# Splitting the first load of a transfer-bound attention-score kernel, and fixed buffers in place of a rotating pool

## The chip, the cores and the metric

The kernel runs on one core of one Trainium2 chip. The metric is the device time of one execution in microseconds; a profile gives, besides, the span from the first to the last instruction, which is about 1.8 us shorter than that time.

## The reference

```python
batch, heads, seq, dim = 8, 8, 512, 64
q, k = float32 [8, 8, 512, 64]
scores = np.einsum('bhqd,bhkd->bhqk', q, k) * (1 / sqrt(64))     # float32 [8, 8, 512, 512]
```

8.4 MB of q and 8.4 MB of k are read, and 67.1 MB of scores are written.

## The kernel before

Four pairs of batches are loaded at the start, k then q, each as one transfer of 128 partitions with 16 KB each (a packet, in what follows, is one such contiguous run). GpSimd casts them to bfloat16 in two halves, TensorE transposes them, and for each pair four output tiles of 4 MB are made by matmuls, evacuated from PSUM (copied out of the buffer into which the matmuls write) by ScalarE and VectorE in turn, and stored. Loads and output tiles share one pool of three buffers of 32 KB a partition.

```python
    big_pool = ctx.enter_context(tc.tile_pool(name="big", bufs=3))
    ...
    def load_and_cast(v):
        xf = big_pool.tile([P, 2, 2, J * D], f32, name="big")
        for x, src in enumerate((k_r, q_r)):
            nc.sync.dma_start(out=xf[:, x], in_=src[v].rearrange("p (s c) -> p s c", s=2))
        for x in range(2):
            xb = bf_pool.tile([P, JP, 2, D, 2], bf16, name="xb")
            for s in range(2):
                pinned(nc.gpsimd.tensor_copy(out=xb[:, :, s]..., in_=xf[:, x, s]...))
    ...
    def scores(v, t):
        o = big_pool.tile([P, 2, RO, S], f32, name="big")
        ...   # 2 x 4 x 2 matmuls, each pair evacuated into o
        nc.sync.dma_start(out=out_r[v, t], in_=o.rearrange("p x i k -> p x (i k)"))
    ...
    cast = [load_and_cast(v) for v in range(UNITS)]        # UNITS = 4: all loads first
```

## Time and profile before

| | before |
|---|---|
| time, median of 6 runs | 202.47 us (202.37 to 202.51) |
| span of the profiled run | 200.7 us |
| transfers: share of the span that the queue's packets took | 98.3% |
| VectorE, TensorE, ScalarE, GpSimd busy | 53%, 52%, 42%, 20% |

Read it from the transfer row: one engine class is full and nothing else is near. The lines themselves stand in the prediction below. "The transfers" are 16 engines side by side, and a share or a GB/s in these views is their mean.

### The profile page before, as it was taken

What the parts mean: (1) busy time and instruction counts of PE and PEld (TensorE: products, weight loads), DVE (VectorE), ACT (ScalarE), POOL (GpSimd) and SP (SyncE); (2) the same over time, 40 slices, a digit from 0 to 9 for tenths busy, and PEclk for the clock granted to TensorE, in tenths of its full rate; (3) what the DMA queues carried; (4) which work ended last, traced back from release to release, by engine and by line L of the source; (5) the groups of instructions that cost most, each with busy time, mean ns of one, the idle gap of its engine ahead of it and who ended that gap; (6) DMA issues with size and microseconds to landing.
All of it is one profiled execution on the core that took longest, in us unless ns stands there. A gap on an engine that the chain in (4) does not pass through costs nothing.

```text
span 200.7 us, 1143 instructions
## 1 busy us (share of the span) xinstructions
PE 105.3 (52%) x384; PEld 45.8 (23%) x384; DVE 106.8 (53%) x98; ACT 85.0 (42%) x97; POOL 39.5 (20%) x22
## 2 busy tenths in 40 slices
PE   0035758566657465478637496748585667510000
PEld 0034535223214131224313122312121111100000
DVE  6705538486475976485749357844444444630000
ACT  2004423864755629253844384366435243620000
POOL 1299999995000000000000000000000000000000
PEclk9999576999699999957999759975858858975555
DMA  6999999999999999999999999999999999999994
GB/s 206 424 444 437 421 421 441 434 395 421 434 424 441 428 431 431 433 426 434 431 428 424 434 441 424 431 431 434 424 431 434 431 424 431 428 437 428 428 428 199
DMA packets 5509, 83.95 MB, mean 418 GB/s; under 512 B 384, under 2 KB 384, under 8 KB 384
## 3 DMA queue, kind: packets, MB, share of 16 engines
q1 hardware_dynamic: 5504, 83.89, 98.3%
q8 instruction: 3, 0.05, 0.1%
q14 instruction: 2, 0.02, 0.0%
HBM read 16.78 MB, written 67.11 MB: 418 GB/s over the span
## 4 chain that ended last, share of the span: by engine, by line
DMA 40%; DVE 10%; PE 8%; ACT 6%; issue 1%; ACTq 0%; SPq 0%; DVEq 0%
DMA out_dram<-big 40%; DVE big L68 9%; PE ps L141 8%; ACT big L66 5%; ACT qz L103 1%; DVE qz L103 1%; ACTq L66 0%; SPq L146 0%; DVEq L68 0%
## 5 line engine op out<-in xcount | busy, mean ns | idle before, releaser
L141 PE MATMUL ps<-kT,qz 128*128 128x512 bf16 x256 | 87.6, 447 | 55.5 <-ACT big L66 41.6
L68 DVE TENSOR_SCALAR big<-ps 128x1024 f32<-128x1024 f32 x64 | 78.4, 1224 | 59.8 <-PE ps L141 37.2
L66 ACT ACTIVATE big<-ps 128x1024 f32<-128x1024 f32 x64 | 65.5, 1023 | 73.0 <-PE ps L141 37.2
L141 PEld LDWEIGHTS <-qz 128*128 128x128 bf16 x256 | 27.2, 106 | 111.0 <-issue 97.5
L89 POOL CAST xb<-big 128x2048 bf16<-128x2048 f32 x16 | 38.8, 2468 | 7.9 <-DMA big<-in_k_dram 7.3
L117 PE MATMUL tp<-identity,xb 128*128 128x128 f32 x64 | 11.6, 346 | 13.4 <-POOL xb L89 13.4
L103 ACT COPY kT<-tp 64x512 f32<-64x512 f32 x16 | 9.2, 577 | 15.3 <-PE tp L117 15.1
L103 DVE COPY kT<-tp 64x512 f32<-64x512 f32 x16 | 11.0, 686 | 6.3 <-PE tp L117 6.0
L117 PEld LDWEIGHTS tp<-identity,xb 128*128 128x128 f32 x64 | 10.5, 184 | 15.2 <-POOL xb L89 13.4
L103 DVE COPY qz<-tp 64x512 f32<-64x512 f32 x16 | 11.0, 687 | 2.7 <-PE tp L125 2.5
L103 ACT COPY qz<-tp 64x512 f32<-64x512 f32 x16 | 9.6, 602 | 2.9 <-PE tp L125 2.7
L125 PE MATMUL tp<-identity,xb 128*128 128x128 f32 x64 | 9.4, 300 | 2.5 <-ACT kT L103 2.5
L125 PEld LDWEIGHTS tp<-identity,xb 128*128 128x128 f32 x64 | 8.5, 156 | 4.3 <-issue 3.3
L156 DVE MEMSET qz<- 128x4096 uint32 x2 | 6.9, 3472 | 2.5 <-PEq L184 1.7
L103 ACT ACT_TABLE_LOAD x1 | 1.3, 1283 | 0.7 <-PEq L184 0.7
masks.py:199 POOL TENSOR_SCALAR_AFFINE_SELECT identity<-identity 128x128 f32<-128x128 f32 x1 | 0.3, 292 | 0.1
masks.py:197 POOL MEMSET identity<- 128x128 f32 x1 | 0.2, 204 | 0.3 <-POOLq L184 0.3
L184 POOL MEMSET const-float32-0.0<- 128x1 f32 x1 | 0.1, 98 | 0.2 <-issue 0.2
L184 POOL MEMSET const-bfloat16-1.0<- 128x1 bf16 x1 | 0.1, 101 | 0.0
L184 POOL MEMSET const-uint8-127<- 128x1 uint8 x1 | 0.1, 101 | 0.0
L184 POOL MEMSET const-float32-1.0<- 128x1 f32 x1 | 0.1, 98 | 0.0
## 6 DMA issues: line engine op xcount, KB each, us to landing
out_dram<-big SPq DMA_DIRECT2D x16, 4096.0 KB, 20.7
big<-in_k_dram SPq DMA_DIRECT2D x4, 2048.0 KB, 18.1
big<-in_q_dram SPq DMA_DIRECT2D x4, 2048.0 KB, 22.7
```

What stands on the lines that cost most here:

```text
L66: pinned(nc.scalar.mul(out=dst, in_=src, mul=scale))
L68: pinned(nc.vector.tensor_scalar(out=dst, in0=src, scalar1=scale, scalar2=None, op0=mybir.AluOpType.mult))
L89: pinned(nc.gpsimd.tensor_copy(out=xb[:, :, s].rearrange("p (g i) d e -> p g e i d", i=wide), in_=xf[:, x, s].rearrange("p (g e i d) -> p ...
L103: pinned(copy(out=dst(s, h), in_=src[:, h]))
L117: pinned(nc.tensor.transpose(out=tp[:, j, :], identity=identity, in_=kb[:, j0 + j]))
L125: pinned(nc.tensor.transpose(out=tp[:, i, jj, :], identity=identity, in_=qb[:, RO * jj + i0 + i]))
L141: pinned(nc.tensor.matmul(out=ps[:, w, :], lhsT=qz[:, i + w, n, :], rhs=kT[:, n].rearrange("d m s j -> d (m s j)"), start=True, stop=True))
L156: nc.vector.memset(qz, 0.0)
L184: nc = _bacc.Bacc("TRN2", target_bir_lowering=False, num_devices=1)
```

## The change

The intent was to let the first cast start after half of the first k load, and to replace whole-slot release by dependences on parts of fixed buffers.

```diff
-    big_pool = ctx.enter_context(tc.tile_pool(name="big", bufs=3))
...
+    n_big = 0
+    def next_big():
+        nonlocal n_big
+        n_big += 1
+        return bigs[(n_big - 1) % 3]
...
-        xf = big_pool.tile([P, 2, 2, J * D], f32, name="big")
+        xf = next_big().rearrange("p (x s c) -> p x s c", x=2, s=2)
         for x, src in enumerate((k_r, q_r)):
-            nc.sync.dma_start(out=xf[:, x], in_=src[v].rearrange("p (s c) -> p s c", s=2))
+            halves = src[v].rearrange("p (s c) -> p s c", s=2)
+            for s in (slice(0, 1), slice(1, 2)) if v == x == 0 else (slice(0, 2),):
+                nc.sync.dma_start(out=xf[:, x, s], in_=halves[:, s])
...
-        o = big_pool.tile([P, 2, RO, S], f32, name="big")
+        o = next_big().rearrange("p (x i k) -> p x i k", x=2, i=RO)
...
+    bigs = [consts.tile([P, 2 * RO * S], f32, name=f"big{n}") for n in range(3)]
```

## The prediction

> **What bounds the kernel now.** I read the page first, its row of slices and its queue table, because a chain of waits has meaning only once one knows whether any engine is full.
>
> ```profile
> span 200.7 us, 1143 instructions
> ...
> DMA  6999999999999999999999999999999999999994
> GB/s 206 424 444 437 421 421 441 434 395 421 434 424 441 428 431 431 433 426 434 431 428 424 434 441 424 431 431 434 424 431 434 431 424 431 428 437 428 428 428 199
> ...
> q1 hardware_dynamic: 5504, 83.89, 98.3%
> ...
> HBM read 16.78 MB, written 67.11 MB: 418 GB/s over the span
> ```
>
> The transfers are full in 38 of 40 slices, and one queue fills 98.3% of the span. No compute engine is above 53%. The traffic is what the reference needs: both inputs once (16.78 MB), the output once (67.11 MB). The change alters none of it. To see what the two open slices hold, I asked for a table of stretches (length, matmul busy time, granted clock, DMA share, GB/s):
>
> ```profile
> core 0: us, PE busy (x), PEclk, DMA share, GB/s
> 0.00:10.00 10.00, 0.00 (x0) 1.00 0.81 315
> 10.00:40.00 30.00, 17.48 (x75) 0.83 1.01 432
> 40.00:50.00 10.00, 6.05 (x31) 1.00 1.01 416
> 50.00:100.00 50.00, 32.22 (x126) 0.90 1.01 430
> 100.00:150.00 50.00, 33.07 (x113) 0.80 1.01 431
> 150.00:195.00 45.00, 16.46 (x46) 0.69 1.01 430
> 195.00:200.70 5.70, 0.00 (x0) 0.50 0.53 227
> ```
>
> The rate is 430 to 432 GB/s wherever the queue is fed. The first 10 us move 3.15 MB, which at 430 is 7.3 us of work: the transfers start, in effect, at 2.7 us. The last 5.7 us move 1.29 MB, 3.0 us of work: they stop, in effect, at 198.0, and 2.7 us of completion and closing waits follow. 40 to 50 us lacks 14 GB/s for 10 us, 0.14 MB or 0.33 us, where loads give way to stores. So the span is 2.7 + 83.95/0.430 (195.2) + 2.7 = 200.6 us against 200.7 measured; the 1.7 us up to the 202.44 us of the timed runs lies outside the span. Only 2.7 us at the front, 0.3 us in the middle and 2.7 us at the end are not transfer.
>
> The chain that ended last and the queue's own waits look different, and would mislead if read alone:
>
> ```profile
> SPq L146 <- DVE big L68: 152.5, 16, 17.6
> SPq L195 <- DMA out_dram<-big: 21.2, 3, 9.6
> SPq L83 <- DMA big<-in_q_dram: 9.5, 1, 9.5
> SPq L83 <- POOL xb L89: 4.9, 1, 4.9
> ```
>
> The issuing queue waits 152.5 us for evacuations, yet each store takes 20.7 us from issue to landing (median, issue table), while its 4.19 MB need 9.75 us at 430 GB/s. About 11 us of that is queueing behind the store before it. The evacuations in turn wait for stores to free a buffer. This is a loop throttled by the transfers, not a slow producer.
>
> **What the Trainium skill says.** "DMA: Bandwidth & Descriptors", section Specifications, puts the ceiling of a core's 16 DMA engines at 435 GB/s, and "Perfetto Trace Analysis", section Roofline, says that a core running alone is bounded by those engines and not by its share of HBM. The trace agrees: 430 to 432 GB/s, with nothing to win above it. The DMA page, section Anatomy of one DMA, makes a transfer's fixed cost (about 2 us, on the GpSimd path) mainly completion latency, not setup; here transfers queued behind one another run at 432 GB/s, so it shows only at the ends. "SBUF — State Buffer", section SBUF: two separate sides, says that VectorE in a two-port mode and GpSimd lock each other out of a shared port for a whole instruction. That matters because GpSimd's casts will now start during VectorE's second memset. In the trace before, cast and memset overlap by 0.8 us (8.58 to 9.40) without either being longer (memset 3.47 us like the first; casts 2447 to 2491 ns), so I expect no lockout.
>
> **The change, part by part.** The opening, from the timeline:
>
> ```profile
> 0.74 0.39 SPq L83 DMA_DIRECT2D big<-in_k_dram  x1
> 1.18 0.42 SPq L83 DMA_DIRECT2D big<-in_q_dram  x1
> ...
> 8.58 34.34 POOL L89 CAST xb<-big 128x2048 bf16<-128x2048 f32 x14 [7.28 <-DMA big<-in_k_dram]
> 13.44 3.28 PEld L117 LDWEIGHTS tp<-identity,xb 128*128 128x128 f32 x16 [13.44 <-POOL xb L89]
> ```
>
> *Split load.* One more issue on the queue, 0.44 us, at 1.2 us, while 1.05 MB (2.44 us) is already queued: hidden. 128 packets of 16 KB become 256 of 8 KB, plus 16 completion packets: 144 more. I estimate 0.1 us from the footnote on the DMA page (Bandwidth section: about 10.5 ns a packet at the floor): 144 x 10.5 ns = 1.5 us, over 16 engines 0.09 us. The first cast moves from 8.58 to about 8.58 - 2.44 = 6.1 us, the second to 8.6 and its end to 11.1 (13.4 before). The q tile, however, lands at 13.4 us before (the queue's 9.5 us wait that follows its issues, which end at 3.9) and still does. GpSimd, which ran without a pause from 8.58 to 42.9, will stop from 11.1 to 13.4, and all its later casts stay put. The k transposes start 2.3 us earlier. The q transposes, which began at 19.61 after the k copies, can begin when q is cast, near 18.4: the first score product comes about 1.2 us earlier, not 2.4. None of it is on the transfer path.
>
> *Persistent buffers.* Three rotating 32 KB buffers before, the same three in the same rotation after, so the capacity in flight is unchanged. What changes is the grain of the dependences: a pool slot is released as a whole, a fixed tile by the part accessed. The built program shows it. The first evacuation into the second buffer waited for all four casts of batch pair 1 (28.13 us in the trace); now it waits for its two k casts, which end near 23.2. The fourth k load waits for the k casts alone, so it can issue near 11 to 13 us instead of 18.33; but six loads of 2.1 MB keep the queue full until 2.7 + 12.6/0.430 = 32 us, so either time is early enough. The first store should leave near 33 instead of 36.81, the second near 43 instead of 47.49, the third near 53 instead of 56.55. The loads end at 2.7 + 16.78/0.430 = 41.7, so even before the first store was 4.9 us early, and the second, needed by 41.7 + 9.75 = 51.5, 4.0 us early. More slack, zero time. After that each store waits for a buffer that the transfers free every 9.75 us, as before. Most evacuations now carry one more wait, on something long past: some tens of ns against 9.75 us per output tile, of which evacuation needs about 8 to 9 (four of 1.02 us on ScalarE beside four of 1.22 us on VectorE, with products between), and 11 us of queue lie in front of it.
>
> Sum: +0.1 for packets, 0 for the split's lead, -0.05 at the turn from loads to stores if it is touched at all, 0 for steady state: 202.44 + 0.05, which I round to 202.4.
>
> **Rivals.** (1) *The head start reaches the end*: 2.4 us of earlier work ends the program 1.2 to 2.4 us sooner, 200.0 to 201.2. For it: the first cast does start with a 7.28 us wait on that load. Against it: the queue is full from 2.7 to 198.0 us; earlier stores only queue longer. (2) *The dip at 40 to 50 us is a late store*, and earlier stores close it: -0.33 us, 202.1. Against: both stores were issued 4 us ahead, so I read the dip as the turn from reads to writes. (3) *Small packets hurt where the queue is empty*: the first packets start with no queue behind them, and the split may lose up to 0.5 us there: 202.9. (4) *The extra waits slow the refill* until a store comes late: it would take over 10 us per tile; at 1 us per tile still nothing. A full loss of 0.3 us on each of 16 stores would be 207, but nothing in the profile speaks for it.
>
> **Range and chances.** The known terms are tenths of a microsecond, the three runs before spread over 0.10 us, and 2% is 4.05 us, more than the front and the middle gap hold together (3.0 us). Rivals 2 and 3 set the range: 201.9 to 202.9. Faster by 2%: 0.01; slower: 0.01; within: 0.98.
>
> **What would show it.** Right: queue share about 98%, 430 GB/s between 50 and 195 us, first cast near 6.1, a GpSimd pause until about 13.4, first store 3 to 5 us earlier, its time to landing longer by as much, last store issued within 0.5 us of 178.1. Wrong: a stretch under 425 GB/s after 50 us (a starved queue), a first packet stretch of clearly under 315 GB/s, or an end of transfers before 197 us, which would mean that the transfer path itself got shorter.

## The result, and the profile after

The changed kernel took 203.31 us (median of 6 runs, 202.74 to 203.79) against 202.47 us (6 runs, 202.37 to 202.51): ratio 1.0043, with a 95% interval of 1.0024 to 1.0061. A ratio here is the mean time of one kernel's fast runs over that of the other's fast runs in the same rounds, so it isn't quite the ratio of the medians. The change is within 2%, as forecast, but it is slower by more than the noise, and outside the stated range of 201.9 to 202.9. Not only the median moved: the six runs spread over 1.05 us, against 0.14 us before.

The profiled run happened to be the fastest of the six (202.74 us, span 200.9). Its page, the rows of slices, packets and queue:

```profile
DMA  6999999999999999999999999999999999999994
GB/s 205 447 427 434 427 434 424 431 372 440 424 431 427 442 424 432 424 437 431 424 431 434 431 434 434 427 427 431 437 431 431 424 434 427 434 421 434 434 431 192
DMA packets 5653, 83.95 MB, mean 418 GB/s; under 512 B 400, under 2 KB 400, under 8 KB 400
...
q1 hardware_dynamic: 5648, 83.89, 98.3%
```

The queue is as full as before. The 5648 packets are 144 more than 5504: 128 for the split and 16 completion records. The ninth slice (40 to 45 us) reads 372 GB/s, where it read 395. The table of stretches, with the same columns as before, says the same:

```profile
0.00:10.00 10.00, 0.00 (x0) 1.00 0.84 324
10.00:40.00 30.00, 18.02 (x86) 0.94 1.01 430
40.00:50.00 10.00, 6.36 (x28) 1.00 0.98 403
50.00:100.00 50.00, 30.35 (x113) 0.86 1.01 431
...
195.00:200.90 5.90, 0.00 (x0) 0.50 0.54 230
```

The front is better than before (324 against 315 GB/s: 0.09 MB, or 0.2 us at 430). The stretch from 40 to 50 us is worse (403 against 416 GB/s: 0.13 MB, or 0.3 us). From 50 to 195 us the rates agree within 1 GB/s. The timeline of the start (start, duration, engine, operation, and the wait in brackets):

```profile
6.10 4.92 POOL L98 CAST xb<-big 128x2048 bf16<-128x2048 f32 x2 [4.80 <-DMA big<-in_k_dram]
...
11.04 0.33 SPq L92 DMA_DIRECT2D big<-in_k_dram  x1
...
13.45 29.46 POOL L98 CAST xb<-big 128x2048 bf16<-128x2048 f32 x12 [2.44 <-DMA big<-in_q_dram]
...
18.34 3.45 PE L134 MATMUL tp<-identity,xb 128*128 128x128 f32 x16 [3.60 <-POOL xb L98]
...
23.20 0.61 PE L150 MATMUL ps<-kT,qz 128*128 128x512 bf16 x2 [1.41 <-DVE qz L112]
...
33.72 17.43 SPq L155 DMA_DIRECT2D out_dram<-big  x3
```

The compute engines did get their head start: first cast at 6.10 us in place of 8.58, a pause of 2.44 us until q lands, first store at 33.72 in place of 36.81. None of it shortened the transfers. And the queue's waits look like before, which again tells nothing:

```profile
SPq L155 <- DVE big L66: 154.4, 16, 15.0
```

So the trace of the fast run explains 0.1 to 0.2 us, and shows a place to look: the turn from loads to stores near 41 us. What the slow runs add had to come from further traces.

**Two measures.** The Trainium skill ("DMA: Bandwidth & Descriptors", section "Why a DMA increments its semaphore by 16 and not by 1") states that a transfer's engines finish independently, and that its semaphore counts them. The page of the profile agrees: 384 packets under 512 bytes before are 24 transfers times 16. These records carry times, so from the packet records of each trace one can read when each of the 16 engines finished each transfer (a record doesn't name its engine). I use two numbers from them:

- *Loss at the last load*: the mean of the 16 finish times of the last load, less that of the load before it, less 4.87 us, which is the spacing of the early loads. Before: 42.24 - 36.98 - 4.87 = 0.39, or 0.40 us with more digits.
- *Lag*: the finish of the slowest engine in the last store, less the mean of the 16. Before: 199.48 - 198.33 = 1.15 us.

The execution ends with the slowest engine: time less its finish is 2.9 to 3.3 us in every trace.

### The profile page after: what moved, and what is told of

Read it like the earlier page. It is cut to its first block, busy times and chain, and to the rows that moved or that the text cites. A ratio compares the mean times of both kernels' runs of the same rounds, so it can differ in the third digit from the quotient of the medians.

```text
span 200.9 us, 1212 instructions
## 1 busy us (share of the span) xinstructions
PE 103.3 (51%) x384; PEld 44.7 (22%) x384; DVE 106.8 (53%) x98; ACT 85.1 (42%) x97; POOL 39.6 (20%) x22
## 3 DMA queue, kind: packets, MB, share of 16 engines
q1 hardware_dynamic: 5648, 83.89, 98.3%
## 4 chain that ended last, share of the span: by engine, by line
DMA 52%; PE 8%; DVE 8%; ACT 6%; issue 1%; ACTq 0%; SPq 0%; DVEq 0%
DMA out_dram<-big 52%; PE ps L150 8%; DVE big L66 7%; ACT big L64 6%; DVE qz L112 1%; DVE kT L112 1%; ACTq L64 0%; SPq L155 0%; DVEq L66 0%
## 5 line engine op out<-in xcount | busy, mean ns | idle before, releaser
L150 PE MATMUL ps<-kT,qz 128*128 128x512 bf16 x256 | 86.6, 440 | 60.6 <-ACT big L64 47.1
L98 POOL CAST xb<-big 128x2048 bf16<-128x2048 f32 x16 | 38.9, 2469 | 8.1 <-DMA big<-in_k_dram 4.8
L126 PE MATMUL tp<-identity,xb 128*128 128x128 f32 x64 | 10.3, 319 | 11.1 <-POOL xb L98 11.1
L126 PEld LDWEIGHTS tp<-identity,xb 128*128 128x128 f32 x64 | 9.4, 169 | 12.5 <-POOL xb L98 11.1
L134 PE MATMUL tp<-identity,xb 128*128 128x128 f32 x64 | 9.7, 306 | 3.6 <-POOL xb L98 3.6
L134 PEld LDWEIGHTS tp<-identity,xb 128*128 128x128 f32 x64 | 8.8, 161 | 5.2 <-POOL xb L98 4.0
L165 DVE MEMSET qz<- 128x4096 uint32 x2 | 6.9, 3472 | 2.5 <-PEq L194 1.7
```

The lines of the kernel that those rows point to most:

```text
L98: pinned(nc.gpsimd.tensor_copy(out=xb[:, :, s].rearrange("p (g i) d e -> p g e i d", i=wide), in_=xf[:, x, s].rearrange("p (g e i d) -> p ...
L126: pinned(nc.tensor.transpose(out=tp[:, j, :], identity=identity, in_=kb[:, j0 + j]))
L134: pinned(nc.tensor.transpose(out=tp[:, i, jj, :], identity=identity, in_=qb[:, RO * jj + i0 + i]))
L150: pinned(nc.tensor.matmul(out=ps[:, w, :], lhsT=qz[:, i + w, n, :], rhs=kT[:, n].rearrange("d m s j -> d (m s j)"), start=True, stop=True))
L165: nc.vector.memset(qz, 0.0)
```

## The experiments

Sixteen runs, each correct. "Loss" and "lag" in this summary are the two measures; GB/s is the 40 to 50 us stretch. Each row is one trace, of a run that took the time in the last column.

| run | ratio (95%) | GB/s | loss us | lag us | traced run us |
|---|---|---|---|---|---|
| before | 1 | 416 | 0.40 | 1.15 | 202.52 |
| before_again | 1.0000 (0.9984 to 1.0016) | 418 | 0.40 | 1.14 | 202.51 |
| fixed_only | 1.0000 (0.9987 to 1.0012) | 416 | 0.41 | 1.19 | 202.61 |
| late_split | 1.0007 (0.9995 to 1.0020) | 419 | 0.24 | 1.16 | 202.60 |
| split_only | 1.0014 (1.0000 to 1.0028) | 403 | 0.72 | 1.02 | 202.64 |
| split_only_again | 1.0026 (1.0011 to 1.0040) | 406 | 0.54 | 1.16 | 202.74 |
| changed kernel | 1.0043 (1.0024 to 1.0061) | 403 | 0.65 | 1.08 | 202.74 |
| after_again | 1.0024 (1.0008 to 1.0040) | 392 | 0.96 | 1.69 | 203.40 |
| after_third | 1.0020 (1.0004 to 1.0036) | 393 | 0.92 | 1.80 | 203.55 |
| no_head | 1.0024 (1.0011 to 1.0038) | 395 | 0.79 | 1.19 | 202.82 |
| tail_split | 1.0029 (1.0014 to 1.0044) | 396 | 1.07 | 1.30 | 203.11 |
| all_split | 1.0028 (1.0015 to 1.0040) | 429 | 0.20 | 1.68 | 203.24 |
| quarters | 1.0042 (1.0030 to 1.0054) | 421 | 0.18 | 1.68 | 203.65 |
| warm_start | 1.0036 (1.0024 to 1.0048) | 423 | 0.22 | 1.33 | 203.25 |
| one_8k | 1.0019 (1.0005 to 1.0033) | 411 | 0.49 | 1.33 | 203.03 |
| part_split | 1.0239 (1.0225 to 1.0253) | 421 | 0.03 | 1.71 | 207.41 |

### First: which part, and is it real

**before_again**, the kernel before against itself. No edit.

> The kernel before against itself, a null: all theories expect 0.9995 to 1.0005 and a spread of 0.1 to 0.2 us. A ratio outside of that would say that differences of 0.4% cannot be read from these comparisons.

Measured: 1.0000; five of its six runs lay from 202.45 to 202.59 us and one at 203.26, and one of the eleven runs beside it took 203.38. So the null holds in the mean, but the kernel before, too, has a rare run 0.8 us longer. The interval of a comparison is about 0.15% either way, and a statement finer than that needs the traces.

**after_again**, the changed kernel unaltered.

> The changed kernel unaltered, for a second sample and a second trace. Theory S (the split load disturbs the transfers at the start) and theory P (the fixed buffers and their earlier first stores disturb the turn from loads to stores) both expect a ratio near 1.004 again and a spread of about 1 us between its runs. Theory N (the first comparison only met a worse moment of the chip) expects 1.000 to 1.001 and a spread of 0.1 to 0.2 us like that of the kernel before.

Measured: 1.0024, six runs from 202.70 to 203.40 us. Theory N, a bad moment of the chip, falls, though the excess is about half of the first one (1.0043).

**fixed_only**, the buffers without the split.

```diff
-            for s in (slice(0, 1), slice(1, 2)) if v == x == 0 else (slice(0, 2),):
+            for s in (slice(0, 2),):
```

> The three fixed buffers alone, the first k load in one transfer. Theory S: 1.000. Theory P: 1.003 to 1.005, with a first store about 3 us earlier and a deeper dip of the rate between 40 and 50 us (403 GB/s as in the changed kernel, against 416). Theory N: 1.000 to 1.001.

Measured: 1.0000, six runs from 202.57 to 202.71 us, 416 GB/s at the turn. Theory P falls: the fixed buffers, with all their further waits, cost nothing that can be measured. The forecast of an earlier first store with this edit alone was too bold: it left at 36.11 us, 0.7 us earlier, not 3.

**split_only**, the rotating pool with the split.

```diff
-            nc.sync.dma_start(out=xf[:, x], in_=src[v].rearrange("p (s c) -> p s c", s=2))
+            halves = src[v].rearrange("p (s c) -> p s c", s=2)
+            for s in (slice(0, 1), slice(1, 2)) if v == x == 0 else (slice(0, 2),):
+                nc.sync.dma_start(out=xf[:, x, s], in_=halves[:, s])
```

> The rotating pool of the kernel before with the split of the first k load alone. Theory S: ratio 1.003 to 1.005, the loss whole. Theory P: 1.000 to 1.001 (0.1 us at most for 144 further packets). Theory N: 1.000 to 1.001.

Measured: 1.0014, less than the 1.003 to 1.005 that theory S expected, but with the dip (403 GB/s). It left open whether the two parts work together. A later pair on one chip answered that.

**after_third** and **split_only_again**, both unaltered.

> The changed kernel once more, beside the split alone on one chip. So far the changed kernel read 1.0024 and 1.0043, the split alone 1.0014, the fixed buffers alone 1.0000. If the split is the whole cause, this and the next run agree within 0.1%; if the two parts work together, this one is 0.1 to 0.2% slower. In the trace: the last load's 16 completions come on average 0.65 us or more later than an undisturbed load takes (0.40 in the unsplit kernels).

> The split alone once more. Split as whole cause: ratio 1.002 to 1.004, as the run before it. Parts together: 1.001 to 1.0015. Loss at the last load 0.65 us or more either way.

Measured: 1.0020 and 1.0026, which agree well within their intervals; the mean times are 203.12 and 203.08 us. (These two are best compared with each other.) The split is the cause as far as these runs resolve, and there is no sign that the buffers add to it. The loss at the last load came out at 0.92 and at 0.54 us; the latter is below the 0.65 us that was expected.

### Second: what about the split

**late_split**: the same two transfers of 8 KB runs, one batch pair later, behind 4 MB of queue.

```diff
-  ... if v == x == 0 else (slice(0, 2),):
+  ... if v == 1 and x == 0 else (slice(0, 2),):
```

> Fixed buffers; not the first k load but that of batch pair 1 is split into two transfers of 8 KB runs, behind 4 MB of queue. Unsplit kernels so far moved 416 to 418 GB/s between 40 and 50 us and split ones 392 to 403. Theory H1 (8 KB runs matter because the queue is empty when they start: they set how the 16 engines stand to each other, and that comes due where loads turn into stores): 414 to 418 GB/s there, ratio 0.999 to 1.001. Theory H2 (one more transfer in the queue): 392 to 405 GB/s, ratio 1.0015 to 1.004. Theory H3 (8 KB packets anywhere ahead of the turn): as H2.

Measured: 1.0007, interval including 1, loss 0.24 us, 419 GB/s. It has as many packets and transfers as the changed kernel, so neither their number (H2) nor 8 KB packets anywhere ahead of the turn (H3) explains the loss by itself. The place of the split matters, then; but the loads also came 0.18 us later here than in the changed kernel (37.07 against 36.89 us, mean finish of the last load but one), to which I return below.

**part_split**: two transfers of 64 partitions with 16 KB runs.

```diff
-                nc.sync.dma_start(out=xf[:, x, s], in_=halves[:, s])
+                nc.sync.dma_start(out=xf[p, x], in_=halves[p])      # p: 0 to 63, then 64 to 127
```

> Fixed buffers; the first k load in two transfers of 64 partitions each, all runs 16 KB. H1: 414 to 418 GB/s between 40 and 50 us, ratio 0.999 to 1.001. H2 (one more transfer): 392 to 405 GB/s, 1.0015 to 1.004. H3: as H1. The first cast has to wait for both transfers, so it starts near 8.6 us.

Measured: 1.0239, far outside all three expectations, and for a reason of its own: 184 GB/s in the first 10 us, loads 4.7 us late. So it tells nothing of the split by 8 KB runs. It does show that cutting a load over partitions was ruinous here where cutting it along them was not.

**one_8k**: one transfer, whose second half lands 64 bytes further on, so that its runs are 8 KB.

```diff
+        if v == 0:
+            gap = bigs[0][:, :2 * (J * D + 16)].rearrange("p (s c) -> p s c", s=2)[:, :, :J * D]
+            ...                                      # q behind it
-                nc.sync.dma_start(out=xf[:, x, s], in_=halves[:, s])
+            nc.sync.dma_start(out=xf[x], in_=halves)
```

> Fixed buffers; the first k load is one transfer, but its second half lands 64 bytes further on, so that its runs are 8 KB as in the changed kernel; the first cast starts near 8.4 us, so there is no head start. H1: 392 to 405 GB/s between 40 and 50 us, ratio 1.0015 to 1.004. H2: 414 to 418, 0.999 to 1.001. H3: as H1. If the head start of the compute engines were the cause (theory C: other addresses in use when the turn comes), 414 to 418 and 1.000.

Measured: 1.0019, 411 GB/s, between the two forecasts. The first packet came at 2.15 us in place of 1.75, and the loads stayed 0.33 us later than in fixed_only (37.33 against 37.00 us, mean finish of the last load but one), which is most of its 0.4 us; the loss is 0.49 us, nearer to the unsplit 0.41 than to the split's 0.54 to 0.96. So 8 KB packets at the start alone, without two transfers, did not bring the whole dip.

**all_split**: all eight loads in two transfers each.

```diff
-            for s in (slice(0, 1), slice(1, 2)) if v == x == 0 else (slice(0, 2),):
+            for s in (slice(0, 1), slice(1, 2)):
```

> Fixed buffers; all eight loads split into two transfers of 8 KB runs, the doses summed. H1: the first split sets the engines as in the changed kernel, the turn loses as much (392 to 405 GB/s), and 7 x 128 further packets add about 0.1 us for each load at the 0.05 to 0.1 us an engine measured for one (7 x 8 packets of 309 ns more against 4 x 611: some 0.4 us): ratio 1.003 to 1.006. H2 and H3: eight times the cause, a turn clearly below 390 GB/s or a ratio above 1.006.

Measured: 1.0028, but no dip (429 GB/s) and a loss of 0.20 us. The time is inside H1's range and the mechanism is not: this run is slow through a lag of 1.68 us, and because the loads are 0.4 us later by then (37.26 against 36.89 in the changed kernel). H1 as stated, "the first split sets the turn", is contradicted.

### Third: the turn itself

**store_late**: no split; the first output goes into the buffer loaded last, so that no store can stand in the queue behind the loads.

```diff
+    n_big = 3  # the first output goes into the buffer that is loaded last
     ts = {}
```

> Fixed buffers, no split; the first output goes into the buffer loaded last, so no store can be issued before about 52 us, long after the loads have landed (42 us), and the queue runs dry for 10 us or more: 212 to 218 us, slower on purpose. It asks whose packets are slow between 38 and 43 us. T1 (stores waiting behind the last load slow it): the last load lands in the undisturbed time, its loss under 0.1 us, against 0.40 us. T2 (the loads are slow there by themselves): 0.3 to 0.5 us is lost as before.

Measured: 212.38 us; the first store was issued at 49.5 us and the loss at the last load was 0.02 us. The stretches around the turn of the kernel before, of after_third and of this run (stretch, its length, granted TensorE clock, DMA share, GB/s counted by the start of packets), in this order:

```profile
38.00:40.00 2.00, 1.00 1.08 451
40.00:42.00 2.00, 1.00 0.93 328
42.00:44.00 2.00, 1.00 1.07 459
```

```profile
38.00:40.00 2.00, 1.00 1.07 410
40.00:42.00 2.00, 1.00 0.90 254
42.00:44.00 2.00, 1.00 0.99 418
```

```profile
38.00:40.00 2.00, 0.50 1.00 426
40.00:42.00 2.00, 0.50 0.83 352
```

In the first two the engines are busy for 90 to 93% of 40 to 42 us and yet start few packets: their packets last longer. In the third, packets keep their length and the share falls merely because the loads are over before 42 us. The packet records say it directly: between 38.8 and 42.3 us the kernel before has 22 packets longer than 660 ns (typical is 611), after_third 36, and they belong to the last load, since the earliest engine finishes that load at 42.0 us before and at 42.2 in after_third. So the last load was slowed with stores waiting behind it, and not here. This doesn't single out the stores: without a free buffer, VectorE and ScalarE stood idle here from 36 to 40.5 us, where they worked in the other two. Nor are waiting stores enough: in part_split the first store waited from 39.83 us, the last load ended at 46.6, and the loss was 0.03 us.

**store_late_split**: the same with the split.

> The changed kernel with the first output in the buffer loaded last, as in the earlier run without the split (212.38 us, 0.02 us lost at the last load). If stores queued behind the last load are needed for the loss, it is below 0.1 us here as well, and the split is no slower: 212.1 to 212.6 us, the loads landing about 0.1 us earlier. If the split slows the last load by itself: 0.3 us or more.

Measured: loss 0.03 us, loads landing 0.10 us earlier, as expected. In this trace the split costs the last load nothing when no store follows. The time was 213.27 us, 0.9 us longer and outside the forecast: the first store landed 0.7 us later (61.12 against 60.39 us, mean of the 16 engines), an effect of where compute stood, which I did not pursue.

**no_head**: the split kept, the head start taken away by casting the second half first.

```diff
-            for s in range(2):
+            for s in ((1, 0) if v == x == 0 else (0, 1)):
```

> The changed kernel, but GpSimd casts the second half of the first k load first, so that it waits for both transfers and starts near 8.4 us: the split stays, the head start of the compute engines goes. Theory H4 (the way in which the 16 transfer engines start on 8 KB packets is what makes the last load slower): loss at the last load 0.54 us or more, ratio 1.002 to 1.004. Theory H6 (the head start shifts the compute engines against the turn): 0.36 to 0.45 us as in the unsplit kernels, ratio 0.999 to 1.001.

Measured: first cast at 8.55 us, loss 0.79 us, 395 GB/s, ratio 1.0024. H6 falls: the head start of the compute engines is not needed for the dearer turn. What this run keeps is the split, and with it the lead of the loads (36.85 us against 36.98 before, mean finish of the last load but one).

**tail_split**: the changed kernel with the last q load split, too.

```diff
-  ... if v == x == 0 else (slice(0, 2),):
+  ... if v == x == 0 or (v, x) == (3, 1) else (slice(0, 2),):
```

> The changed kernel with the last q load split into two transfers of 8 KB runs as well. The kernel with all loads split lost only 0.20 us at the last load. If the loss at the turn is what the change costs, the loss falls to 0.25 us or less here and the ratio to 1.000 to 1.001; if it comes from elsewhere (the slowest engine's drift later), the ratio stays at 1.002 to 1.004 whatever the turn does.

Measured: loss 1.07 us, ratio 1.0029. Smaller packets in the last load do not cure the turn; the expectation failed, and with it my reading of all_split.

**quarters**: four transfers of 4 KB runs; **warm_start**: unsplit, behind a load of 128 runs of 512 bytes that nothing reads.

```diff
+                for n in range(4):                      # quarters: C = 1024 columns
+                    nc.sync.dma_start(out=xf[:, 0, n // 2, n % 2 * C:(n % 2 + 1) * C], in_=...)
+    nc.sync.dma_start(out=warm, in_=q_r[0][:, :128])    # warm_start
```

> The first k load in four transfers of 4 KB runs. H4: loss at the last load 0.65 us or more, ratio 1.003 to 1.005, and loads that reach 37 us as early as, or earlier than, with two. H6: like the changed kernel with its head start, 1.002 to 1.004. A loss of 0.45 us or less would contradict both.

> Fixed buffers, no split; a load of 128 runs of 512 bytes into a buffer that nothing reads goes ahead of the first k load. Everything moves by about 0.45 us (one issue) at most, ratio up to 1.002 for that alone. H4 in its general form (small packets first let the engines start differently): loss at the last load 0.54 us or more, ratio 1.003 to 1.006. If only 8 KB packets of the load itself do it: 0.36 to 0.45 us and 1.000 to 1.002.

Measured: ratios 1.0042 and 1.0036, but losses of 0.18 and 0.22 us. Both are slow because their loads are 0.5 us late from the start (37.54 and 37.51 us against 37.00 in fixed_only), quarters in addition through a lag of 1.68 us. H4, that small packets at the start make the turn dearer, is contradicted by both as stated, though their total times would have passed for confirmation.

One thing orders nearly all of these losses, and no run was made to test it: when the loads arrive. Sorted by the mean finish of the last load but one, the loss falls from 1.07 us in tail_split (36.70 us) over 0.92 in after_third (36.82), 0.65 in the changed kernel (36.89), 0.40 before (36.98) and 0.24 in late_split (37.07) to 0.20 in all_split (37.26), 0.22 in warm_start (37.51) and 0.18 in quarters (37.54). The other traces with early stores fit in within 0.02 us, but for one_8k (37.33, loss 0.49). An earlier arrival by itself raises this measure by as much; from 36.98 to 36.70 us, 0.28 us, it rises by 0.67. Two traces speak against the split as such: all_split and quarters split the first load and lose little. Since late_split, quarters and warm_start moved the loads as well as the packets, they speak against H2 to H4 only if the time of arrival doesn't matter, and no run here separates the two.

### Fourth: where the rest of a slow run is

A dearer turn of 0.14 to 0.56 us doesn't fill a run that takes 203.55. The last microseconds of the kernel before and of after_third, the same columns:

```profile
197.00:198.00 1.00, 0.50 0.77 328
198.00:199.00 1.00, 0.50 0.27 115
199.00:200.00 1.00, 0.50 0.00 0
```

```profile
197.00:198.00 1.00, 0.50 0.92 393
198.00:199.00 1.00, 0.50 0.31 131
199.00:200.00 1.00, 0.50 0.08 33
```

In after_third packets are still started after 199 us at 33 GB/s, which in 1 us is two packets of 16 KB. The records place them at 199.19 and 199.80 us, one behind the other on one engine; the other fifteen are done by 199.52, this one at 200.41. Against before_again (202.51 us) the sum is: mean finish 198.61 - 198.34 = 0.27 us, lag 1.80 - 1.14 = 0.66 us, together 0.93 of the 1.04 us between the two times. The lag did not arise at the turn: the distance between first and last engine was 1.61 us in the stores that landed from 52 to 91 us, and grew by about 0.1 us a store from some 110 us on, to 2.57 us. after_again shows the same growth, all_split and quarters as well; in after_again, whose slowest engine I followed packet by packet, its packets last 614 to 634 ns for stretches of several us in place of 611. The fast traces of the split kernels (202.64 to 202.82 us) have lags of 1.02 to 1.19 us, like the unsplit ones.

Yet the growth itself is not peculiar to slow runs. In each of the sixteen traces with early stores, the kernel before included, exactly one engine falls further behind the median engine from store to store: by 0.58 to 0.67 us over the four stores from the one that lands near 101 us to the one near 140. The traces differ in where that engine stands at 101 us. In after_again, after_third, all_split and quarters it is already 0.92 to 1.08 us behind (1.00 in part_split, where this store lands at 105 us), in all the others 0.27 to 0.74 us (0.59 before). There the fall stays nearly hidden, because other engines are 1.1 to 1.5 us behind for another reason (last section).

## Why the prediction was wrong, point by point

**What bounds the kernel** was right: the transfers, at 430 GB/s from 50 to 195 us before and after. Rival 1, the head start, was rightly rejected: first cast and first store came 2.5 and 3.1 us earlier and the time did not fall.

**Fixed buffers at no cost** was right (fixed_only 1.0000), and so was rejecting rival 4.

**No lockout between GpSimd and VectorE** was right: the casts from 6.10 us ran beside the second memset, with 2469 ns on average, and the memset took 3472 ns, both as before. That this memset works in the two-port mode to which the prediction referred, no run shows.

**The head start's details** were mostly right: first cast 6.10 (6.1 stated), pause to 13.45 (13.4), q transposes at 18.34 (18.4), first three stores at 33.72, 42.90 and 50.78 (33, 43, 53). The first product came 0.37 us earlier, not 1.2: the 16 q transposes took 3.45 us in place of 2.57. The last store was issued at 179.83 us, not within 0.5 us of 178.1, without consequence, since it was still queued for 20 us.

**The cost of 144 packets, 0.1 us**, was of the right size: an 8 KB packet lasts 309 ns, so two take 7 ns longer than one of 16 KB, and eight such pairs an engine come to 0.06 us. That was luck: the 10.5 ns of "DMA: Bandwidth & Descriptors" (section Bandwidth) is the whole time of a small transfer shared out over its 64 packets, not what a further packet costs one engine, so dividing it by 16 engines again had no ground. At the front, where rival 3 feared a loss of up to 0.5 us, the split even gained: the loads ran 0.1 to 0.2 us ahead.

**The step that failed** is in the sum, in two of its terms. The first is "0 for the split's lead, -0.05 at the turn from loads to stores if it is touched at all". The turn was touched, in the other direction. The four unsplit or late-split traces lost 0.24 to 0.41 us there; the six with the first load in two transfers and no other edit to the loads lost 0.54 to 0.96. Part of that is their lead handed back: in the mean of the engines the last store ended 0.09 to 0.27 us later than before. I had seen the dip and read it rightly as the turn itself and not a late store, but then treated its size as fixed. This alone doesn't leave the stated range: the split traces with an ordinary lag took 202.64 to 202.82 us.

The second is "0 for steady state". The sum carried one transfer path at its mean rate, and the program waits for the slowest of 16 engines. In the two slow traces of the changed kernel the lag was 1.69 and 1.80 us in place of 1.14, grown while the mean rate stayed at 430 to 431 GB/s, and it was the larger term (in after_third 0.66 us against 0.27). The range, built on a spread of 0.10 us in three runs, had no room for it. (The sum was also rounded wrongly: 202.44 + 0.05 is 202.5, not 202.4. Nothing rests on it.)

**What stays open.** It is shown that the split and not the buffers costs the time, and that the turn is dearer in the six traces where it is the only edit to the loads. The same split further back did not do this, and the head start of the compute engines is not needed for it. The loss was gone in the two without stores behind the loads, where compute idled, too. It is not shown why. A split first load alone is not enough (all_split and quarters), and number and size of packets, the count of transfers, and small packets first fell as stated, but with loads that arrived at other times; the time of arrival is the rival left untested. Nor is it shown why one engine falls back in every trace, or what sets where it stands at 101 us. Slow runs were far commoner with the split (13 of the 18 runs of the changed kernel took over 203 us, against 2 of 43 of the kernel before), but a trace of a slow run of the kernel before was not caught, so what made those two slow is not known. No variant beat the kernel before.

## What to carry to other kernels

The transfers were full from start to end here: starting compute earlier bought nothing, and cutting the first transfer cost a little: judge it by the end of the loads and by the finish of the slowest transfer engine, not by the first cast. The mean rate hid 1 to 1.8 us of lag among 16 engines here; read the completion records of the last transfer before working out a sum to a tenth of a microsecond. And look at the mechanism of an experiment as well as at its time: three variants here had the time that a theory forecast and a different cause.

## What the Trainium skill lacked or had wrong

- "DMA: Bandwidth & Descriptors": nothing on the turn from loads to stores in one queue. The last load lost 0.40 us with stores behind it and 0.02 us without.
- The same page, Latency and other measured facts, calls two engines usually slower and, as a best guess, ties this to GpSimd's path. Here all transfers came from the SP queue, and the slowest of 16 engines still ended 1.0 to 1.8 us after the mean.
- "Runtime: NRT & Kernel Launch" has a section on instruction fetches, but neither it nor the DMA page says what one costs the kernel's own transfers. The line "q8 instruction: 3, 0.05" on the page of the kernel before stands for three packets of 16 KB; the first, at 48.4 us, lasted 0.96 us, and the slowest engine finished the first store at 53.38 us where the median engine finished at 51.96; I take the packet for the reason. After the second packet (98.9 us) two engines, at 101 us, were 1.3 to 1.4 us behind the median, where there had been one. Every trace of a kernel with early stores shows a first such packet between 43 and 50 us, so it doesn't explain the difference.
- The DMA page, section Bandwidth, gives about 10.5 ns a packet as the floor of a 4 KB transfer of 64 packets, and no cost for large packets. Here two packets of 8 KB took 7 ns longer than one of 16 KB.
